# Matmul with batch normalisation on one core: the contraction dimension dealt to partitions in runs of eight, and the weight loaded block by block

## The chip, the core and the metric

The kernel runs on one core of one Trainium2 chip. The metric is the device time of one execution in microseconds (us), as the median of several runs. Before the change it is 205.72 us (three runs, 205.65 to 206.19).

Five engines work side by side: TensorE (PE, with its weight loads shown apart as PEld), VectorE (DVE), ScalarE (ACT), GpSimd (POOL) and SyncE (SP). Each works through its own queue of instructions in order. POOL and SP also issue the DMA transfers.

## The reference

```
y    = np.matmul(x, weight)            # x: 16 x 512 x 1024, weight: 1024 x 768, float32
mean = np.mean(y, axis=(0, 1), keepdims=True)
var  = np.var(y, axis=(0, 1), keepdims=True)
out  = gamma * (y - mean) / np.sqrt(var + eps) + beta
```

So 8192 rows of 1024 numbers (k) are multiplied by a 1024 x 768 matrix, and each of the 768 columns is normalised by its own mean and variance over all 8192 rows. No output can leave before the statistics of its column are complete.

## The kernel before

**Tiling.** The 8192 rows are 16 chunks of 512 (CH); a half chunk is 256 rows (QR). The contraction of 1024 is cut into 8 steps of 128 partitions: four blocks jw (JW = 4), each with two parities e. The 768 columns are six groups nt of 128. For nt 0 and 1 the product is made with rows on partitions (`rows_unit`, matmuls of line 510: x is the stationary operand, 256 columns of w move). For nt 2 to 5 it is made with columns on partitions (`col_unit`, line 575: w is stationary, x moves).

**How x gets its layout.** x comes in float32 and is cast to bf16 by the transfers that POOL issues (`load_x`, line 403): four transfers for each load, one for each quarter i of k, into partitions 32i to 32i+31 of the buffer `ring`. Each partition then holds 256 consecutive k of some rows. DVE transposes blocks of 32 x 32 (`turn_x`). For most chunks it moves pairs of bf16 numbers as one float32 word (line 435); for chunks 2, 3 and 6 (SINGLE) it moves single bf16 numbers and parts the two parities (line 428). Afterwards partition 32i + c holds k = 256 i + 64 jw + 2 c + e. In the source of the transpose the words of one block lie side by side (index c has step one word); for SINGLE the step of c is two bf16 numbers, also four bytes.

**How w gets its layout.** w must follow the same assignment of k. Since 32i + c maps to 256 i + ..., one transfer can fill only 32 partitions: `load_quarter` (line 387) loads quarter i of two blocks. There are eight such transfers: quarters 0 and 1 of blocks 0 and 1 first (`BETWEEN`, issued inside the first load of x), then the four transfers of x's rows 0 to 255, quarters 2 and 3 of blocks 0 and 1, x's rows 256 to 511, and the four quarters of blocks 2 and 3. Ahead of it, SP fetches one number from each of several rows of w (`touched`, line 350).

**The order around the change.** The order of instructions on every engine is made by a planner (`arrange`) that runs when the kernel is built. Every piece of work is a task with a due time, a modelled cost and its dependencies. The loads stand in the list `order` (line 440), and a POOL transfer waits until one of eight completion lanes is free. On PE the first chunk is taken in pieces: `part(0, 1, [0, 1])` multiplies rows 0 to 255 with blocks 0 and 1 (8 matmuls of line 510 and 16 of line 575); then one idle matmul pair (`FILL`, `wake`, line 591); then `part(1, 2, [0, 1])` the same for rows 256 to 511; then blocks 2 and 3 for all 512 rows. `WAKE` idle matmuls run before that from 1.5 us on. In the first chunk the transposes are split in two, blocks 0 and 1 and blocks 2 and 3.

**What follows.** From chunk 1 on each chunk takes 32 matmuls of line 510 and 32 of line 575, until the column groups are put off for some chunks. The sums of the row form are made by ACT (line 659, squares; line 672, the copy), DVE (line 662, sums; part of line 666) and POOL (the rest of line 666, sums of squares). The column form has its statistics in line 711 (DVE) and its copy in line 715 (ACT).

Of the kernel before, what the change touches and what calls it, by code (L numbers as in the profile page):

```python
# [227 lines left out]
def kernel(  # L228
# [9 lines left out]
    nc = tc.nc  # L238
# [5 lines left out]
    B, M0, K = x.shape  # L244
# [4 lines left out]
    NT = N // P  # L249
    KQ = K // 4  # L250
    CH = 512
# [4 lines left out]
    JW = KQ // 64  # L256
    PIECES = ((0,QR),(QR,QR))
    WAKE = 8
    FILL = 1
    SMALL = 8  # L260
    TOUCH = 1
    BETWEEN = {0: [0, 1]}
    EARLY = 4
    SHORT = 2
    GA = 2
# [27 lines left out]
    def seq(bi):  # L293

        ins = bi.ins
        prev = last.get(ins.engine)
        if prev is not None:
            tc.add_manual_dep(
                ins, prev,
                mybir.DependencyInfo(mybir.DependencyClass.NoSync, mybir.DependencyReason.DATA),  # L300
                reason="order",
            )
        last[ins.engine] = ins.name
        return bi
# [40 lines left out]

    seq(nc.scalar.activation(warm, eps_sb, AF.Sqrt))
    touched = singles.tile([P, 2, TOUCH], f32)
    first_rows = weight.rearrange("(i jw c e) n -> i c jw (e n)", i=4, jw=JW, e=2)
    for i in range(4):
        seq(nc.sync.dma_start(touched[32 * i:32 * i + 32, 0:2], first_rows[i, :, 0:2, 0:TOUCH]))  # L350


    tasks, turns = [], {}
# [2 lines left out]
    def task(prio, engines, emit, deps=(), lock=False, **kw):  # L356
        t = Task(prio, engines, emit, deps, **kw)
        t.lock = lock
        tasks.append(t)
        return t  # L360
# [19 lines left out]

    w_ready, x_ready, x_slot, plain, last_loads = {}, {}, {}, {}, []

    w_rows = weight.rearrange("(i jw c e) n -> i c jw (e n)", i=4, jw=JW, e=2)
    w_flat = w_sb.rearrange("p jw e n -> p jw (e n)")

    def load_quarter(i, jw, jw1):
        seq(nc.gpsimd.dma_start(w_flat[32 * i:32 * i + 32, jw:jw1], w_rows[i, :, jw:jw1]))  # L387

    def load_w(jw, jw1, quarters):
        def emit(eng):  # L390
            for i in quarters:
                load_quarter(i, jw, jw1)
        return emit

    def load_x(m0, rows, slot, between):
        def emit(eng):
            x_bf = piece(slot).bitcast(bf16).rearrange("p (t k) -> p t k", k=KQ)
            slot.tile = x_bf
            src = x_flat[m0:m0 + rows].rearrange("(t r) k -> r t k", r=32)
            for i in range(4):  # L400
                for quarter in between.get(i, ()):
                    load_quarter(quarter, 0, 2)
                bi = seq(nc.gpsimd.dma_start(x_bf[32 * i:32 * i + 32], src[:, :, KQ * i:KQ * (i + 1)]))  # L403
            slot.loader.ins = bi.ins
        return emit
# [11 lines left out]
    def turn_x(xslot, slot, m0, t0, jw0, jw1, new, rows=QR):  # L417
        def emit(eng):
            single = m0 // CH in SINGLE
            if new:  # L420
                xT_sb = xtpool.tile([P, JW, 2, CH] if single else [P, JW, CH, 2], bf16, tag="xT")
                slot.tile = xT_sb
            half, row = divmod((m0 + 32 * t0) % CH, QR)
            if single:
                src = xslot.tile[:, t0:t0 + rows // 32].rearrange("p t (jw c e) -> p t jw e c", jw=JW, e=2)
                dst = slot.tile[:, :, :, half * QR + row:half * QR + row + rows]
                dst = dst.rearrange("p jw e (t r) -> p t jw e r", r=32)
                seq(nc.vector.transpose(dst[:, :, jw0:jw1], src[:, :, jw0:jw1]))  # L428
                return
            src = xslot.tile[:, t0:t0 + rows // 32].rearrange("p t k -> p (t k)").bitcast(f32)  # L430
            src = src.rearrange("p (t jw c) -> p t jw c", jw=JW, c=32)
            dst = slot.tile.rearrange("p jw m e -> p (jw m e)").bitcast(f32)
            dst = dst.rearrange("p (jw q t r) -> p q t jw r", jw=JW, q=QPC, r=32)
            dst = dst[:, half, row // 32:(row + rows) // 32, jw0:jw1]
            seq(nc.vector.transpose(dst, src[:, :, jw0:jw1]))  # L435
        return emit

    for c in range(C):
        x_slot[c] = Slot(xts)
    order = [("x", 0), ("w", 0, 2), ("x", 1), ("w", 2, 4)]  # L440
    order += [("x", q) for q in range(2, SHORT * QPC)] + [("c", c) for c in range(SHORT, C - 1)]
    at = M - CH
    for rows in (CH-P,P):
# [3 lines left out]
    affine = None  # L447
    for kind, n, *n1 in order:
        if kind == "w":
            quarters = [i for i in range(4) if n > 0 or i not in sum(BETWEEN.values(), [])]  # L450
            took = len(quarters) * 192 * 4 * (n1[0] - n) / 4 * PER_KB * 1.024
            w_ready[n] = task(t, {"POOL": (0.535 * len(quarters), 0.535 * len(quarters))}, load_w(n, *n1, quarters), dma=took)
            w_ready[n].count = len(quarters)
            t += 2.1 * (n1[0] - n)
            if n1[0] == JW:
                idt = task(t, {"POOL": (0.6, 0.6)}, lambda eng: make_identity(nc, ident))
                task(t, act(0.25), lambda eng: seq(nc.scalar.copy(ident32, ident)), [idt])
            continue
        rows = n1[0] if kind == "p" else QR if kind == "x" else CH
        m0 = n if kind == "p" else n * rows  # L460
        if m0 == M // 2:
            affine_loads = affine = task(t, {"SP": (5.0, 7.0)}, load_affine, [x_ready[m0 // CH - 3, 0, JW]])
        slot = Slot(rings, rows // 32 * KQ // 2)
        between = BETWEEN if m0 == 0 else {}
        also = sum(len(v) for v in between.values())
        load = task(
            t, {"POOL": (2.68 * rows / CH + 0.535 * also, 2.68 * rows / CH + 0.535 * also)}, load_x(m0, rows, slot, between),
            dma=(rows * K * 4 / 1024 + 384 * also) * PER_KB * 1.024, takes=[slot])
        load.count = 4 + also
        slot.loader = load  # L470
        last_loads.append(load)
        t += 2.7 * rows / QR
        for i in range(rows // QR):
            c, q = divmod(m0 // QR + i, QPC)
            for j0, j1 in ((0, JW // 2), (JW // 2, JW)) if m0 < CH else ((0, JW),):
                new = q == 0 and j0 == 0
                x_ready[c, q, j1] = task(
                    -1000 + t, dve((2.2 if c in SINGLE else 1.16) * (j1 - j0) / JW + 0.02),
                    turn_x(slot, x_slot[c], m0, i * QR // 32, j0, j1, new), [load],
                    uses=[slot] if new else [slot, x_slot[c]], takes=[x_slot[c]] if new else [])  # L480
                if not new:
                    x_ready[c, q, j1].deps.append(x_ready[c, 0, JW // 2 if m0 < CH else JW])
            x_ready.setdefault((c, q, JW // 2), x_ready[c, q, JW])
        if rows % QR:
            t0 = rows // QR * QR // 32
            m1 = m0 + 32 * t0
            c, q = divmod(m1 // QR, QPC)
            x_ready["tile", m1 // P] = task(
                -1000 + t, dve(0.63), turn_x(slot, x_slot[c], m0, t0, 0, JW, False, P),
                [load, x_ready[c, 0, JW]], uses=[slot, x_slot[c]])  # L490
            x_ready[c, q, JW] = x_ready[c, q, JW // 2] = x_ready["tile", m1 // P]
# [95 lines left out]
    def wake(count, slot):  # L587
        def emit(eng):
            idle_ps = psum.tile([P, CH], f32, tag="b")
            for _ in range(count):  # L590
                seq(nc.tensor.matmul(idle_ps, idle_sb[:, 0:P], idle_sb, start=True, stop=True))  # L591
            small = idle_sb[:, 0:P // 2].bitcast(bf16)
            for _ in range(SMALL if count == WAKE else 0):
                seq(nc.tensor.matmul(idle_ps[:, 0:P], small, small, start=True, stop=True))
        return emit
# [5 lines left out]
    def pe_task(occ, emit, deps, key=None, **kw):  # L601
        t = task(clock[0], pe(occ), emit, deps, **kw)
        t.after = begun.get(key)
        begun[key] = t if key else None
        emit.task = t
        clock[0] += occ
        return t
# [166 lines left out]
    def part(q0, q1, jws):  # L774
        for h in range(q0, q1):
            rows_unit(0, [2 * h, 2 * h + 1], jws)
        for nt in range(GA, NT):
            col_unit(nt, 0, jws, q0, q1)

    part(0, 1, [0, 1])  # L780
    fill_slot = Slot(banks)
    pe_task(0.87 * FILL, wake(FILL, fill_slot), [w_ready[0]], takes=[fill_slot])
    part(1, 2, [0, 1])
    for h in range(2):
        rows_unit(0, [2 * h, 2 * h + 1], [2, 3])
    for nt in range(GA, NT):
        col_unit(nt, 0, [2, 3])

    halves = [range(JW // 2), range(JW // 2, JW)]
    merges = []  # L790
# [621 lines left out]
```

## Time and profile before

| | |
|---|---|
| median of three runs | 205.72 us (205.65 to 206.19) |
| span of the profiled execution, first to last instruction | 204.1 us |
| the rest of the median around that span | 1.6 us |
| mean granted PE clock over the span | 0.979 of full speed |
| HBM traffic | 36.71 MB read, 25.17 MB written |
| all loads of x have landed at about | 100 us |

The profile is of one execution; its time is given by its span, and the time around the span is taken as the difference to the median. "Busy" is the time in which an engine worked on an instruction. The chain of waits follows the last instruction back to what released it, step by step. "Releaser" is what ended an idle time. A transfer's "landing" is counted from its issue.

### The profile page before, as it was taken

The numbers are of one execution on the slowest core, as the hardware profiler recorded it, in microseconds if no ns is written. First come the engines' busy times: TensorE is split into PE (matmuls) and PEld (weight loads), VectorE is DVE, ScalarE is ACT, GpSimd is POOL, SyncE is SP. The second block draws the span as 40 slices with busy tenths as digits, with TensorE's granted clock in tenths as the row PEclk, the third lists the DMA queues.
The fourth block names the chain that finished last, engine by engine and source line by source line (L and its number), as shares of the span: only waits on it lengthen the run. The fifth ranks groups of instructions, "written<-read, shape, count | busy, mean of one in ns | idle before, by whom it ended". The sixth has DMA issues, their size and how long they took to land.

```text
span 204.1 us, 3510 instructions
## 1 busy us (share of the span) xinstructions
PE 189.3 (93%) x1210; PEld 114.5 (56%) x1210; DVE 159.3 (78%) x250; ACT 146.2 (72%) x260; POOL 124.1 (61%) x150
## 2 busy tenths in 40 slices
PE   7969999999999999999999999999999999997900
PEld 3457554657488888777865444444444445544600
DVE  4031879999999999969989998987999878657900
ACT  2001461368989999899978766999998959956950
POOL 7776954877499989997403999389613312940000
PEclk9999999999999999999999999999999999999965
DMA  4999999999999999999686899899999999999998
GB/s 71 172 199 196 176 196 196 196 197 197 190 193 197 197 196 196 196 197 195 103 181 200 297 339 336 248 301 328 295 322 227 336 303 274 347 343 310 310 347 253
DMA packets 98562, 48.74 MB, mean 239 GB/s; under 512 B 24304, under 2 KB 98032, under 8 KB 98544
## 3 DMA queue, kind: packets, MB, share of 16 engines
q0 software_dynamic: 34624, 18.36, 65.5%
q1 hardware_dynamic: 63920, 30.16, 52.6%
q8 instruction: 9, 0.15, 0.3%
q14 instruction: 9, 0.07, 0.1%
HBM read 36.71 MB, written 25.17 MB: 303 GB/s over the span
## 4 chain that ended last, share of the span: by engine, by line
PE 86%; ACT 3%; DMA 3%; POOL 2%; issue 1%; ACTq 0%; DVE 0%; POOLq 0%
PE y_ps L575 54%; PE y_ps L510 24%; PE y_ps L814 4%; ACT o_sb L1361 3%; DMA ring<-in_x_dram 3%; PE o_ps L1044 1%; POOL ring L403 1%; POOL w_sb L387 1%; PE y_ps L753 1%; PE a_ps L903 1%; PE o_ps L1074 0%; ACTq L1407 0%; PE idle_ps L591 0%; PE tot_ps L871 0%; ACT ring L1252 0%
## 5 line engine op out<-in xcount | busy, mean ns | idle before, releaser
L575 PEld LDWEIGHTS <-w_sb 128*128 128x128 bf16 x520 | 50.3, 97 | 57.6
L575 PE MATMUL y_ps<-xT_sb,w_sb 128*128 128x512 bf16 (+1 forms) x272 | 59.3, 371 | 0.0
L575 PE MATMUL y_ps<-x_pl,w_sb 128*128 128x512 bf16 x248 | 57.4, 379 | 0.0
L403 POOL DMA_DIRECT2D ring<-in_x_dram x76 | 47.2, 626 | 14.4 <-DMA ring<-in_x_dram 5.5
L510 PE MATMUL y_ps<-w_sb,xT_sb 128*128 128x256 bf16 x448 | 50.6, 273 | 1.7 <-DMA ring<-in_x_dram 1.6
L510 PEld LDWEIGHTS <-xT_sb 128*128 128x128 bf16 x448 | 43.5, 98 | 9.4 <-DVE xT_sb L435 2.9
L435 DVE STREAM_TRANSPOSE xT_sb<-ring 128x1024 f32<-128x1024 f32 (+1 forms) x29 | 31.2, 1111 | 14.1 <-DMA ring<-in_x_dram 13.9
L711 DVE BATCH_NORM_STATS2 stats<-y_ps 128x6 f32<-128x512 f32 x46 | 30.9, 687 | 7.7 <-PE y_ps L575 7.2
L715 ACT CAST y_sb<-y_ps 128x512 bf16<-128x512 f32 x51 | 29.0, 593 | 10.4 <-DVE stats L711 6.3
L547 ACT COPY x_pl<-xT_sb 128x1024 bf16<-128x1024 bf16 x32 | 32.8, 1063 | 1.7 <-DVE xT_sb L435 1.7
L942 POOL TENSOR_TENSOR ring<-ring,sum 128x1024 f32<-128x1024 f32 (+1 forms) x11 | 23.8, 2188 | 14.9 <-ACT y_ps L724 10.9
L659 ACT ACTIVATE sq_sb<-y_ps 128x512 f32<-128x512 f32 x28 | 16.3, 610 | 16.2 <-PE y_ps L510 15.9
L666 POOL TENSOR_TENSOR sum<-sum,sq_sb 128x512 f32<-128x512 f32 x20 | 25.6, 1278 | 3.0 <-ACT sq_sb L659 1.7
L662 DVE TENSOR_TENSOR sum<-y_ps,sum 128x512 f32<-128x512 f32 x28 | 18.9, 675 | 6.3 <-ACT sq_sb L659 5.3
L672 ACT CAST y_sb<-y_ps 128x512 bf16<-128x512 f32 x28 | 16.3, 594 | 8.2 <-DVE sum L662 8.0
L1178 POOL TENSOR_TENSOR ring<-ring,sum 128x1024 f32<-128x1024 f32 x6 | 14.8, 2477 | 9.8 <-issue 8.5
L937 DVE TENSOR_TENSOR ring<-y_sb,a_ps 128x1024 f32<-128x1024 bf16 (+1 forms) x16 | 16.7, 1079 | 0.1
L1044 PE MATMUL o_ps<-ident,y_sb 128*128 128x128 bf16 x104 | 13.1, 221 | 1.6 <-DVE y_sb L1348 1.5
L1232 ACT CAST ring<-ring 128x1024 f32<-128x1024 bf16 x13 | 13.8, 1063 | 0.6 <-DMA ring<-y_sb 0.6
L1145 POOL COPY sum<-sum 32x256 f32<-32x256 f32 (+1 forms) x17 | 5.8, 340 | 13.4 <-DVE sum L1142 6.5
L428 DVE STREAM_TRANSPOSE xT_sb<-ring 128x2048 bf16<-128x2048 bf16 x6 | 13.5, 2290 | 0.1
L591 PE MATMUL idle_ps<-idle_sb 128*128 128x512 f32 x18 | 9.6, 688 | 1.5 <-DVE idle_sb L316 1.5
(104 smaller groups left out, 153.7 us busy)
## 6 DMA issues: line engine op xcount, KB each, us to landing
out_dram<-ring SPq DMA_DIRECT2D x37, 512.0 KB, 3.4
ring<-in_x_dram POOLq DMA_DIRECT2D x52, 256.0 KB, 8.8
out_dram<-o_sb SPq DMA_DIRECT2D x6, 512.0 KB, 4.7
ring<-in_x_dram POOLq DMA_DIRECT2D x16, 128.0 KB, 5.9
w_sb<-in_weight_dram POOLq DMA_DIRECT2D x8, 192.0 KB, 6.2
out_dram<-ring SPq DMA_DIRECT2D x6, 256.0 KB, 3.0
ring<-in_x_dram POOLq DMA_DIRECT2D x4, 192.0 KB, 7.8
out_dram<-o_sb SPq DMA_DIRECT2D x3, 256.0 KB, 2.5
```

The source lines that it names most:

```text
L403: bi = seq(nc.gpsimd.dma_start(x_bf[32 * i:32 * i + 32], src[:, :, KQ * i:KQ * (i + 1)]))
L435: seq(nc.vector.transpose(dst, src[:, :, jw0:jw1]))
L510: seq(nc.tensor.matmul(y_ps[:, s], x_of(c, jw, e, t * P, (t + 1) * P), w_sb[:, jw, e, 0:NA], start=(s == 0 and jw == 0 and e == 0), stop=( ...
L547: seq(nc.scalar.copy(dst, pairs) if eng == "ACT" else ENG[eng].tensor_copy(dst, pairs))
L575: seq(nc.tensor.matmul(y_ps, w_sb[:, jw, e, nt * P:(nt + 1) * P], moving(c, jw, e, q0 * QR, q1 * QR, parted), start=(jw == 0 and e == 0 an ...
L659: seq(nc.scalar.activation(sq_sb[:, 0:n], slot.tile[:, 0:n], AF.Square))
L662: seq(nc.vector.tensor_add(sum1, slot.tile[:, 0:n], sum1))
L666: seq(ENG[eng].tensor_add(acc, acc, state["sq"][:, 0:n]))
L711: seq(nc.vector.bn_stats(dst, slot.tile))
L715: seq(nc.scalar.copy(y(nt, c), slot.tile))
L937: seq(nc.vector.tensor_mul(slot.o, y_row[c].y[:, s0:s1], aff[0][:, None, :].to_broadcast([P, n, NA])))
L942: seq(ENG[eng].tensor_add(slot.o, slot.o, row[:, None, :].to_broadcast([P, n, NA])))
```

## The change

k is dealt out anew: partition p holds k = 8 p + 2 jw + e. For w that gives every partition eight consecutive rows of the matrix, and a block jw is two of them, 6 KB in one piece. One transfer with all 128 partitions loads one block, and there are four such transfers. For x the transfers stay as they are, since 8 p with p = 32 i + c is 256 i + 8 c. The transposes pick other words: the index c now has a step of four words (16 bytes), or of eight bf16 numbers (16 bytes) in the SINGLE chunks. What they write is laid out as before.

The list of loads becomes block 0, x rows 0 to 255, block 1, x rows 256 to 511, block 2, block 3. PE takes rows 0 to 255 with block 0 and then with block 1, rows 256 to 511 with both, and then block 2 and block 3 each for all 512 rows. The idle pair between the parts is gone.

```
-    first_rows = weight.rearrange("(i jw c e) n -> i c jw (e n)", i=4, jw=JW, e=2)
+    w_rows = weight.rearrange("(p jw e) n -> p jw (e n)", jw=JW, e=2)
...
-    def load_quarter(i, jw, jw1):
-        seq(nc.gpsimd.dma_start(w_flat[32 * i:32 * i + 32, jw:jw1], w_rows[i, :, jw:jw1]))
-
-    def load_w(jw, jw1, quarters):
-        def emit(eng):
-            for i in quarters:
-                load_quarter(i, jw, jw1)
+    def load_w(jw):
+        def emit(eng):
+            seq(nc.gpsimd.dma_start(w_flat[:, jw], w_rows[:, jw]))
...
-                for quarter in between.get(i, ()):
-                    load_quarter(quarter, 0, 2)
...
-                src = xslot.tile[:, t0:t0 + rows // 32].rearrange("p t (jw c e) -> p t jw e c", jw=JW, e=2)
+                src = xslot.tile[:, t0:t0 + rows // 32].rearrange("p t (c jw e) -> p t jw e c", jw=JW, e=2)
...
-            src = src.rearrange("p (t jw c) -> p t jw c", jw=JW, c=32)
+            src = src.rearrange("p (t c jw) -> p t jw c", jw=JW, c=32)
...
-    order = [("x", 0), ("w", 0, 2), ("x", 1), ("w", 2, 4)]
+    order = [("w", 0), ("x", 0), ("w", 1), ("x", 1), ("w", 2), ("w", 3)]
...
-    part(0, 1, [0, 1])
-    fill_slot = Slot(banks)
-    pe_task(0.87 * FILL, wake(FILL, fill_slot), [w_ready[0]], takes=[fill_slot])
+    part(0, 1, [0])
+    part(0, 1, [1])
     part(1, 2, [0, 1])
-    for h in range(2):
-        rows_unit(0, [2 * h, 2 * h + 1], [2, 3])
-    for nt in range(GA, NT):
-        col_unit(nt, 0, [2, 3])
+    for jw in range(2, JW):
+        for h in range(2):
+            rows_unit(0, [2 * h, 2 * h + 1], [jw])
+        for nt in range(GA, NT):
+            col_unit(nt, 0, [jw])
```

The planner's cost for a transpose is left as it was. Its plan changes with the new tasks: two of DVE's additions of squares (line 666) go to POOL, POOL makes the identity matrix after the loads of x's rows 256 to 511 and not before them, and the order of statistics, copies and transposes shifts on DVE and ACT until about the last loads of x. After that, and on SP throughout, the order is the same.

## Prediction

> **What bounds it now.** I read the page first, then the windows, the chain of waits and the timeline of the first 30 us.
>
> ```profile
> span 204.1 us, 3510 instructions
> PE 189.3 (93%) x1210; PEld 114.5 (56%) x1210; DVE 159.3 (78%) x250; ACT 146.2 (72%) x260; POOL 124.1 (61%) x150
> ```
>
> The second line is from part 1 of the page: PE is busy 93% of the span. The window from 20 to 101 us says where it is not idle at all (columns: PE, PEld, DVE, ACT, POOL busy, each with its instructions, clock, DMA share, GB/s):
>
> ```profile
> 20.00:101.00 81.00, 80.94 (x600) 58.18 (x599) 74.69 (x87) 63.78 (x106) 65.03 (x86) 1.00 1.43 189
> ```
>
> PE lacks 0.06 us of 81, at full clock. DVE is the next one, with 6.3 us to spare. So a change at the start gains what it lets PE begin *without a break* earlier, and nothing after that. The timeline of the start shows what sets this point:
>
> ```profile
> 10.26 1.30 DVE L435 STREAM_TRANSPOSE xT_sb<-ring 128x512 f32<-128x512 f32 x2 [7.13 <-DMA ring<-in_x_dram]
> ...
> 12.14 1.03 PE L510 MATMUL y_ps<-w_sb,xT_sb 128*128 128x256 bf16 x8 [1.58 <-DMA ring<-in_x_dram]
> ...
> 14.85 1.30 DVE L435 STREAM_TRANSPOSE xT_sb<-ring 128x512 f32<-128x512 f32 x2 [3.28 <-DMA ring<-in_x_dram]
> 15.62 0.82 PEld L510 LDWEIGHTS <-xT_sb 128*128 128x128 bf16 x8 [0.60 <-DVE xT_sb L435]
> ...
> 18.58 1.66 PEld L510 LDWEIGHTS <-xT_sb 128*128 128x128 bf16 x16 [0.33 <-issue]
> ...
> 24.62 1.25 DVE L435 STREAM_TRANSPOSE xT_sb<-ring 128x1024 f32<-128x1024 f32 x1 [0.69 <-DMA ring<-in_x_dram]
> ...
> 25.92 1.64 PEld L510 LDWEIGHTS <-xT_sb 128*128 128x128 bf16 x16 [0.33 <-DVE xT_sb L435]
> ```
>
> Four gates follow each other. (1) 12.14: x's first rows were transposed from 10.26 on, but the last quarter of blocks 0 and 1, issued at 5.32 and landing 6.7 later, came at 12.0. (2) 15.62: rows 256 to 511 had landed at 14.8, and DVE needed 0.65 for half of them. (3) 18.58: the last quarter of blocks 2 and 3, issued at 12.29 with 6.2 to landing, came at 18.5. (4) 25.92: chunk 1's second half landed at 24.5 (issued 18.75, 5.7 to landing) and was transposed by 25.87. The chain of waits has "issue" for 0.07 us at 18.54 and 0.04 at 25.89: gates (3) and (4) are only just gates. The transfers themselves flow without a hole between 7 and 22 us:
>
> ```profile
> GB/s 0 0 31 111 206 152 91 180 206 209 189 194 193 218 217 203 202 186 190 194 193 192 144 171 179 196 197 196 195 196 196 196 195 197 196 197 196 196 198 195
> ```
>
> That is the DMA view of 0 to 40 us, 1 us a number (bytes written).
>
> **The change, step by step.** *Bytes and their order.* Block 0 (384 KB written) takes the place of the first two quarters of blocks 0 and 1 (part 6 of the page: 192 KB each); block 1 that of the next two; blocks 2 and 3 that of the last four. Each load thus ends at the same byte of the stream, and as the stream has no hole, at the same time: block 0 at 6.0 (2.0 issued + 4.0), x's first rows at 10.2, block 1 at 12.0, rows 256 to 511 at 14.8, block 2 at about 16.6, block 3 at 18.5, chunk 1 at 24.5. *Issue.* Eight transfers of w at 534 ns (the first 682) become four; 128 runs each lie between the 64 of a quarter (534) and the 256 of an x load (575), say 0.55. POOL saves 4.4 − 2.3 = 2.1 us by 13 us, hidden behind the stream. POOL makes the identity later (0.5 us); ACT's copy of it waits longer, but behind it stands only line 659, due at 21.6. The two additions that go to POOL stand ahead of chunk 3's loads, which go from 23.4 to about 25; in the stream chunk 2 lasts until 29.7. On SP the four small fetches (1.81 us) stay, and nothing is behind them.
>
> *PE.* Gate (1) becomes 10.26 + 0.65 = 10.95. Block 0 with the first rows is 12 matmuls, half of 0.87 + 1.81 (the rows of the chain for 8 and 16): 1.34, to 12.3; block 1 is there at 12.1; to 13.65. In the kernel before this part ends at 14.85, so 1.2 us are gained there. Gate (2) stays at 15.6 for want of x: the 1.2 us become idle time, 13.65 to 15.6, where the idle pair (0.86) stood. Then 2.68 to 18.35. Gate (3) goes, since block 2 is there since 16.6: 0.2 gained. Blocks 2 and 3 take (1.76 + 3.61) = 5.4, to 23.7; the first half of chunk 1 1.76, to 25.5; then gate (4), at 25.92 as before. The 0.4 us gained turn into a wait there. Sum on the path: **0.0 us**. What stands behind gate (4) on PE is all the rest, so from there on the runs are equal. The statistics of chunk 0 come nearer together (rows end at 21.5 and not 19.5), and about 0.7 us of DVE's sums go past 21.5; DVE is idle 2.3 us between 20 and 40, and PE needs no bank before 27.7.
>
> *The transposes.* They read words 16 bytes apart where the words lay side by side. No row shows such a read. The nearest rows, from the groups by shape up to 105 us:
>
> ```profile
> L435 DVE STREAM_TRANSPOSE xT_sb<-ring 128x1024 f32<-128x1024 f32 x23 | 27.4, 1224 | 3.7 <-DMA ring<-in_x_dram 3.5
> ...
> L428 DVE STREAM_TRANSPOSE xT_sb<-ring 128x2048 bf16<-128x2048 bf16 x6 | 13.5, 2290 | 0.1
> ...
> L435 DVE STREAM_TRANSPOSE xT_sb<-ring 128x512 f32<-128x512 f32 x6 | 3.9, 680 | 10.4 <-DMA ring<-in_x_dram 10.4
> ```
>
> (1224 − 680) / 512 = 1.06 ns an element for words side by side, and 2290 / 2048 = 1.12 for half words picked four bytes apart: the time goes by elements, whether or not the neighbours are wanted. That excludes a gain. I take **no change**, by line 428. The far ends: one more element time for each element, or (time by the bytes passed over) four times. There are 38,912 elements, 41.3 us: the ends are +41 and +124 us of DVE work. Of a doubling, 2.2 us fall on x's first rows, where DVE is idle (0.5 of it on the path); of the other 39.2, DVE's idle time from 20 to 102 us (its windows are busy 17.72 of 20, 18.86 of 20, 22.96 of 24 and 16.04 of 18: 6.4 idle) and the 1.5 us of additions given to POOL can take at most 7.9.
>
> **The rivals.** *The step is paid (slower).* If a word from another 16-byte stretch each time costs DVE twice, DVE takes over as the bound from 25 us on: 39.2 − 7.9 + 0.5 = 32, so **238 us**, and up to 245 if the idle time can't be used. It decides from a fifth on (7.9 of 39.2): below that it hides, at a third more it costs 12.9 − 7.9 = 5, 211 us. For it: DVE is busy 74.7 of 81 us, so there's hardly cover. Against it: line 428 pays nothing for skipping. The Trainium skill, "Advanced Engine Details and Errata", section Memory Cachelines, speaks for it: SBUF has lines of 16 bytes, two hits on a line are needed to absorb the access latency, and a different line at each access costs. No run here shows that: both transposes of the trace read four times from each 16 bytes, so it neither agrees nor differs.
>
> *The clock falls in the idle time.* Without the pair, PE rests 1.95 us. The break of 1.58 us before 12.14 left the clock at 1.00, but after the last matmul (ends 194.1) it fell inside this window:
>
> ```profile
> 194.00:196.00 2.00, 0.09 (x2) 0.00 (x0) 0.00 (x0) 2.00 (x4) 0.00 (x0) 0.92 1.15 346
> ```
>
> 0.92 as a mean of 1 and 0.5 over 2 us puts the fall at 195.7, some 1.6 us after. At the start the weight loads of the idle matmuls (timeline) follow at 0.86 us until 4.2 and at 0.43 from 4.8 on, so from 1.49 on it took about 3 us of work to get the clock up. Price: 3 us at half speed lose 1.5, less the 0.4 in hand at gate (4): +1.1, **206.8**. By the Trainium skill, "TensorE: Matmul & The Clock Gate", Part 1, it takes an idle window of about 3.4 us, and 1.95 would not do; the tail of this trace differs, with a fall 1.6 us after the last matmul.
>
> *The stream comes earlier.* At 5 and 6 us it moves 152 and 91 GB/s where 200 is usual: 157 KB, 0.8 us. If transfers over all 128 partitions fill this dip, every gate comes 0.8 us earlier: **204.9**. Against it: in the dip x's first rows are moved, whose transfers stay as they are.
>
> **How the numbers follow.** Forecast, the stream is the gate as before: 205.72 + 0.0 = 205.7, own range 205.1 to 206.3, chance 0.44. The profiled span of 204.1 should come again; the 1.6 us around it are the difference to the median. The step paid in full 0.32 (238 to 245), in part 0.06 (about 211), the clock 0.08 (206.8), the earlier stream 0.10 (204.9). A measurement of this kernel can tell about 0.3%, 0.6 us, from no change. Faster by more: 0.10 and 0.02 of the forecast's edge, 0.12. Within: 0.39. Slower: 0.32 + 0.06 + 0.08 + 0.03 = 0.49. Signs are thus nearly even, with one case likeliest and another far away. The range takes in all but the ends, 0.06 above and 0.04 below: 204.8 to 243.
>
> **What would show it.** Right: PE's first matmuls near 10.95, an idle time near 13.7 to 15.6 released by DVE, no wait at 18.4, a wait at about 25.5 to 25.9, and PE's window from 26 to 101 as full as before; the 128x1024 transposes near 1224 ns and the bf16 ones near 2290. Wrong: these rows at 2300 and 4460 with PE waiting for line 435 all through (the step is paid); a granted clock below 1 between 13 and 22 us; loads of x landing before 14.2 and 24.0. What I hold for surest is that the loads of x, not w, gate PE from 15 us on; what I know least is the price of the 16-byte step, and it alone could move the time by more than 2 us.

## The result and the profile after

The changed kernel takes 228.62 us (median of four runs, 228.54 to 228.86) beside 205.78 for the kernel before on the same chip: a ratio of 1.1104, interval 1.1076 to 1.1132. It is slower by 22.8 us. The profiled execution agrees: its span is 226.8 us where it was 204.1, 22.7 more. Line numbers of the changed kernel are lower: nine less in the loads and transposes, 14 less from line 510 on (435 is now 426, 428 is 419, 510 is 496, 575 is 561, 662 is 648, 666 is 652, 715 is 701, 403 is 394).

Part 1 of the page after:

```profile
span 226.8 us, 3499 instructions
PE 197.0 (87%) x1208; PEld 115.9 (51%) x1208; DVE 186.3 (82%) x248; ACT 147.2 (65%) x260; POOL 124.9 (55%) x148
```

DVE works 27.0 us longer (159.3 before) with two instructions fewer. PE shows 7.7 us more for the same work less one idle pair, and is idle 29.8 us instead of 14.8. The windows after say where (columns as before: PE, PEld, DVE, ACT, POOL busy, each with its instructions, clock, DMA share, GB/s):

```profile
20.00:40.00 20.00, 17.87 (x114) 10.73 (x113) 17.59 (x14) 7.54 (x14) 13.00 (x17) 1.00 1.37 184
40.00:60.00 20.00, 16.46 (x89) 8.76 (x87) 19.90 (x18) 8.66 (x14) 11.96 (x17) 0.91 1.17 150
60.00:84.00 24.00, 21.09 (x163) 16.52 (x162) 23.69 (x20) 16.93 (x28) 15.16 (x19) 0.93 1.19 144
84.00:102.00 18.00, 13.83 (x107) 10.86 (x106) 17.47 (x16) 13.89 (x22) 13.91 (x16) 0.91 1.29 164
102.00:126.00 24.00, 21.08 (x157) 14.51 (x154) 23.70 (x25) 19.71 (x37) 13.64 (x21) 1.00 0.98 148
```

PE was full from 20 to 101 us; now it lacks 15.7 us of the 106 between 20 and 126, while DVE lacks 3.7 and is full from 40 us on. The bound has changed hands. It is the transposes that grew, as the groups by shape up to 130 us show (count, busy us, mean ns, idle time before):

```profile
L426 DVE STREAM_TRANSPOSE xT_sb<-ring 128x1024 f32<-128x1024 f32 x23 | 46.1, 2043 | 4.5 <-DMA ring<-in_x_dram 4.5
L419 DVE STREAM_TRANSPOSE xT_sb<-ring 128x2048 bf16<-128x2048 bf16 x6 | 22.9, 3872 | 0.0
...
L426 DVE STREAM_TRANSPOSE xT_sb<-ring 128x512 f32<-128x512 f32 x6 | 6.2, 1071 | 9.4 <-DMA ring<-in_x_dram 9.4
```

1224 ns became 2043, 2290 became 3872, 680 became 1071. By (2043 − 1071) / 512 an element now costs 1.90 ns where it cost 1.06. In all DVE has 23 x 0.819 + 6 x 1.582 + 6 x 0.391 = 30.7 us more to do. (The 27.0 of the page is less: DVE makes two additions fewer, and where two rows overlap, as 83.22 + 4.06 and 87.19 below, the page counts that time once.) One stretch of DVE's timeline shows the new rhythm (start, length, engine and line, what it writes and reads, count):

```profile
83.22 4.06 DVE L426 STREAM_TRANSPOSE xT_sb<-ring 128x1024 f32<-128x1024 f32 x2
87.19 2.25 DVE L648 TENSOR_TENSOR sum<-y_ps,sum 128x512 f32<-128x512 f32 x3
89.35 0.68 DVE L652 TENSOR_TENSOR sum<-sum,sq_sb 128x512 f32<-128x512 f32 x1
89.95 3.98 DVE L426 STREAM_TRANSPOSE xT_sb<-ring 128x1024 f32<-128x1024 f32 x2
```

One chunk costs DVE 6.7 us, with no hole. With the old transposes the same work would take 2 x 1.22 + 2.25 + 0.68 = 5.4 us, while two chunks on PE lay 5.65 us apart in the kernel before at this place (rows of line 510 began at 85.41 and 91.06). So PE, which used to set the pace by a little, now waits. The chain that ended last, by engine, says the same (PE had 86% of it before):

```profile
PE 39%; DVE 28%; DMA 12%; issue 11%; ACT 4%; POOL 2%; ACTq 0%; DVEq 0%; POOLq 0%
```

DVE's share is the transposes and sums of that rhythm. In the waits from 10 to 130 us (engine, line, what it waits for: us, times, longest) PE's weight loads and its matmuls wait for line 426; and POOL's loads of x wait too, because the buffer `ring` comes free late, so that the transfers thin out (150 and 144 GB/s from 40 to 84 us in the windows above, 194 and 196 before):

```profile
POOL ring L394 <- DVE xT_sb L419: 15.2, 3, 6.3
...
PEld L496 <- DVE xT_sb L426: 10.2, 8, 3.1
...
PE y_ps L496 <- DVE xT_sb L426: 7.7, 5, 2.8
```

The start, which most of the prediction was about, went nearly as it said (timeline of the start, after):

```profile
11.78 0.60 PE L496 MATMUL y_ps<-w_sb,xT_sb 128*128 128x256 bf16 x4
...
14.62 2.06 DVE L426 STREAM_TRANSPOSE xT_sb<-ring 128x512 f32<-128x512 f32 x2 [2.40 <-DMA ring<-in_x_dram]
15.76 1.05 PE L496 MATMUL y_ps<-w_sb,xT_sb 128*128 128x256 bf16 x8 [1.13 <-DVE xT_sb L426]
...
25.08 2.00 DVE L426 STREAM_TRANSPOSE xT_sb<-ring 128x1024 f32<-128x1024 f32 x1
27.14 1.92 PE L496 MATMUL y_ps<-w_sb,xT_sb 128*128 128x256 bf16 x16 [1.42 <-DVE xT_sb L426]
```

x's rows 256 to 511 landed at 14.5 (forecast 14.8), block 3 of w at 18.3 (18.5), chunk 1's second half at 24.4 (24.5). The third gate, the wait at 18.5, is gone. The rest of the start is the longer transposes again: chunk 1's second half is transposed at 27.08, not 25.87.

### The profile page after: what moved, and what is told of

Same layout as the page of the kernel before. It is cut to its first block, busy times and chain, and to the rows that moved or that the text cites. A ratio compares the mean times of both kernels' runs of the same rounds, so it can differ in the third digit from the quotient of the medians.

```text
span 226.8 us, 3499 instructions
## 1 busy us (share of the span) xinstructions
PE 197.0 (87%) x1208; PEld 115.9 (51%) x1208; DVE 186.3 (82%) x248; ACT 147.2 (65%) x260; POOL 124.9 (55%) x148
## 4 chain that ended last, share of the span: by engine, by line
PE 39%; DVE 28%; DMA 12%; issue 11%; ACT 4%; POOL 2%; ACTq 0%; DVEq 0%; POOLq 0%
PE y_ps L561 34%; DVE xT_sb L426 15%; DMA ring<-in_x_dram 8%; DVE xT_sb L419 5%; DVE sum L648 4%; DMA w_sb<-in_weight_dram 4%; ACT o_sb L1347 3%; PE y_ps L800 2%; DVE sum L652 1%; PE o_ps L1030 1%; DVE stats L697 1%; POOL ring L394 1%; PE y_ps L739 1%; ACT y_sb L701 1%; POOL w_sb L385 1%
## 5 line engine op out<-in xcount | busy, mean ns | idle before, releaser
L496 PE MATMUL y_ps<-w_sb,xT_sb 128*128 128x256 bf16 x448 | 55.5, 283 | 12.8 <-DVE xT_sb L426 7.7
L426 DVE STREAM_TRANSPOSE xT_sb<-ring 128x1024 f32<-128x1024 f32 (+1 forms) x29 | 52.2, 1842 | 13.9 <-DMA ring<-in_x_dram 13.9
L561 PE MATMUL y_ps<-xT_sb,w_sb 128*128 128x512 bf16 (+1 forms) x272 | 61.3, 377 | 2.2 <-ACT y_sb L701 2.2
L496 PEld LDWEIGHTS <-xT_sb 128*128 128x128 bf16 x448 | 44.7, 102 | 24.2 <-DVE xT_sb L426 10.2
L652 POOL TENSOR_TENSOR sum<-sum,sq_sb 128x512 f32<-128x512 f32 x22 | 28.2, 1280 | 9.7 <-ACT sq_sb L645 9.0
L928 POOL TENSOR_TENSOR ring<-ring,sum 128x1024 f32<-128x1024 f32 (+1 forms) x11 | 23.7, 2194 | 17.4 <-ACT y_ps L710 13.3
L658 ACT CAST y_sb<-y_ps 128x512 bf16<-128x512 f32 x28 | 16.4, 587 | 14.2 <-DVE sum L648 14.0
L419 DVE STREAM_TRANSPOSE xT_sb<-ring 128x2048 bf16<-128x2048 bf16 x6 | 22.9, 3872 | 0.0
L1030 PE MATMUL o_ps<-ident,y_sb 128*128 128x128 bf16 x104 | 13.1, 221 | 1.6 <-DVE y_sb L1334 1.5
```

The costliest lines, as they stand in the source:

```text
L496: seq(nc.tensor.matmul(y_ps[:, s], x_of(c, jw, e, t * P, (t + 1) * P), w_sb[:, jw, e, 0:NA], start=(s == 0 and jw == 0 and e == 0), stop=( ...
L561: seq(nc.tensor.matmul(y_ps, w_sb[:, jw, e, nt * P:(nt + 1) * P], moving(c, jw, e, q0 * QR, q1 * QR, parted), start=(jw == 0 and e == 0 an ...
L652: seq(ENG[eng].tensor_add(acc, acc, state["sq"][:, 0:n]))
L928: seq(ENG[eng].tensor_add(slot.o, slot.o, row[:, None, :].to_broadcast([P, n, NA])))
```

## The experiments

The theory: the whole loss is the price of reading words 16 bytes apart, paid on DVE, which has no room for it. The rivals: that the price depends on how far the step goes (bytes passed over), or on what else uses SBUF at the time; that the four transfers of w and the new order have a part in the loss; and that PE's lower granted clock (0.91 to 0.93 from 40 to 102 us) carries some of it.

### The step by itself

A kernel that holds only transposes and copies of 1024 elements, in which the step of the reads goes from 4 to 64 bytes; in the rows shown below one instruction runs after the other, with all else at rest:

```diff
+    nc.vector.transpose(to_f32, f32_at(1))  # f32 read step 4 bytes
+    nc.vector.transpose(to_f32, f32_at(2))  # f32 read step 8 bytes
+    nc.vector.transpose(to_f32, f32_at(3))  # f32 read step 12 bytes
+    nc.vector.transpose(to_f32, f32_at(4))  # f32 read step 16 bytes
...
+    nc.vector.transpose(to_f32, f32_at(16))  # f32 read step 64 bytes
...
```

> Leaves the whole computation out: it only times transposes of 1024 elements (and plain copies on DVE, ACT and POOL) from SBUF, one after the other, with the read step varied; the output is constant. Theory 1 (DVE pays for a new 16-byte stretch of SBUF at each element): float32 transposes at steps of 4 and 8 bytes take 1.06 ns an element above the fixed 0.14 us (about 1.22 us), at 16 bytes and all wider steps the same 1.9 ns (about 2.04 us), 12 bytes in between; bf16 at 4 bytes as at 2, at 16 bytes 1.84 ns. Theory 2 (time goes by the bytes passed over): 8 bytes about 1.5 us, 16 bytes 2.04, 32 bytes 3.7, 64 bytes 7. Theory 3 (what is paid is not the step but the load on SBUF from PE, ACT and DMA in the full kernel): here, with those engines idle, 16 bytes costs 1.22 us as well.

Its timeline, of one execution (each form stands in the kernel twice, and the two agree within 0.1 us; shown is the second. Lines 82 to 84 read bf16 at steps of 4, 8 and 16 bytes; 72 to 75 read float32 at 4, 8, 12 and 16 bytes, 78 at 64; 87 and 90 are DVE's copy at 4 and 16, 93 and 96 ACT's, 99 and 102 POOL's):

```profile
51.40 1.19 DVE L82 STREAM_TRANSPOSE to_bf<-words 128x1024 bf16<-128x1024 bf16 x1
...
53.09 1.22 DVE L83 STREAM_TRANSPOSE to_bf<-words 128x1024 bf16<-128x1024 bf16 x1
...
54.82 1.95 DVE L84 STREAM_TRANSPOSE to_bf<-words 128x1024 bf16<-128x1024 bf16 x1
...
80.75 1.25 DVE L72 STREAM_TRANSPOSE to_f<-words 128x1024 f32<-128x1024 f32 x1 [16.60 <-POOL to_f L71]
82.03 1.25 DVE L73 STREAM_TRANSPOSE to_f<-words 128x1024 f32<-128x1024 f32 x1
83.31 1.53 DVE L74 STREAM_TRANSPOSE to_f<-words 128x1024 f32<-128x1024 f32 x1
84.87 1.98 DVE L75 STREAM_TRANSPOSE to_f<-words 128x1024 f32<-128x1024 f32 x1
...
90.95 1.90 DVE L78 STREAM_TRANSPOSE to_f<-words 128x1024 f32<-128x1024 f32 x1
...
96.18 0.69 DVE L87 COPY to_f<-words 128x1024 f32<-128x1024 f32 x1
...
98.51 1.07 DVE L90 COPY to_f<-words 128x1024 f32<-128x1024 f32 x1
...
100.73 1.04 ACT L93 COPY to_f<-words 128x1024 f32<-128x1024 f32 x1 [27.98 <-DVE to_f L91]
...
104.53 1.99 ACT L96 COPY to_f<-words 128x1024 f32<-128x1024 f32 x1
...
108.64 1.04 POOL L99 COPY to_f<-words 128x1024 f32<-128x1024 f32 x1 [27.92 <-ACT to_f L97]
...
112.48 1.99 POOL L102 COPY to_f<-words 128x1024 f32<-128x1024 f32 x1
```

DVE's transpose pays nothing at 8 bytes, a part at 12, everything at 16, and no more at 64. bf16 does the same by bytes, not by elements: 1.19 us at 4 bytes, 1.22 at 8, 1.95 at 16. So it is neither the distance nor the number of elements skipped, nor traffic of others, since there was none. What fits is the count of numbers taken from each stretch of 16 bytes: two are enough, one costs. The price is not DVE's alone: ACT and POOL pay 0.95 us for 1024 elements as well. A step of 32 bytes in what a transpose writes costs as much (2.00, line 86).

The Trainium skill, "Advanced Engine Details and Errata", section Memory Cachelines, says this: lines of 16 bytes, and two hits on a line to absorb the latency. This run agrees (1.25 at 8 bytes, 1.98 at 16). The price here is 0.73 us for 1024 elements.

### The step alone in the kernel

The kernel before with the two lines that choose the words, and nothing else of the change:

```diff
-                src = xslot.tile[:, t0:t0 + rows // 32].rearrange("p t (jw c e) -> p t jw e c", jw=JW, e=2)
+                src = xslot.tile[:, t0:t0 + rows // 32].rearrange("p t (c jw e) -> p t jw e c", jw=JW, e=2)
...
-            src = src.rearrange("p (t jw c) -> p t jw c", jw=JW, c=32)
+            src = src.rearrange("p (t c jw) -> p t jw c", jw=JW, c=32)
```

> The kernel before with the two lines of the transposes changed alone: they read words 16 bytes apart, and so x's numbers meet the wrong rows of w; loads, their order and PE's order are those of before. Theory 1 (the step alone): 128x1024 transposes at 2.04 us, bf16 at 3.87, and the time of the changed kernel, 227 to 230 us. Theory 2 (the new loads, the PE order and its idle time take part, with the clock): the step by itself gives 215 to 224 us. Theory 3 of the probe (load on SBUF from the 128-partition transfers): close to 206.

228.48 us (228.34 to 228.49), ratio 1.1101 (1.1085 to 1.1118), which is the whole change's ratio. Its groups by shape:

```profile
L435 DVE STREAM_TRANSPOSE xT_sb<-ring 128x1024 f32<-128x1024 f32 x23 | 46.0, 2033 | 0.0
...
L428 DVE STREAM_TRANSPOSE xT_sb<-ring 128x2048 bf16<-128x2048 bf16 x6 | 22.9, 3848 | 0.0
```

### Everything but the step

The kernel after with the old reading, so that its order of instructions is that of the kernel after on every engine:

```diff
-                src = xslot.tile[:, t0:t0 + rows // 32].rearrange("p t (c jw e) -> p t jw e c", jw=JW, e=2)
+                src = xslot.tile[:, t0:t0 + rows // 32].rearrange("p t (jw c e) -> p t jw e c", jw=JW, e=2)
...
-            src = src.rearrange("p (t c jw) -> p t jw c", jw=JW, c=32)
+            src = src.rearrange("p (t jw c) -> p t jw c", jw=JW, c=32)
```

> The changed kernel with the old reading of the transposes: words side by side, so x's numbers meet the wrong rows of w; loads by block, PE's order and the removed idle pair are those of the change. Theory 1: transposes at 1.22 and 2.29 us, gates as the prediction had them (first matmuls near 10.95 us, an idle time from 13.7 to 15.6, chunk 1's second half near 25.9), and 205.7 us, within 0.6 of before. Theory 2: 208 us or more, with the granted clock under 1 between 13 and 22 us or PE idle after 26 us.

205.98 us (205.54 to 206.48), ratio 1.001 (1.000 to 1.0021), span 204.0. This is the prediction's forecast of no change, met by all of the change but the step. Its timeline of the start has the gates as they were forecast, at 10.95, 15.6 and 25.9:

```profile
11.15 0.60 PE L496 MATMUL y_ps<-w_sb,xT_sb 128*128 128x256 bf16 x4
...
15.27 1.05 PE L496 MATMUL y_ps<-w_sb,xT_sb 128*128 128x256 bf16 x8 [1.27 <-DVE xT_sb L426]
...
25.76 1.92 PE L496 MATMUL y_ps<-w_sb,xT_sb 128*128 128x256 bf16 x16 [0.53 <-DVE xT_sb L426]
```

At 11.15 PE came from its own idle matmuls, though: x's first rows were transposed by 10.65. There is no wait at 18, PE is full from 40 to 102, and the clock is 1.00 from 10 to 20 us. So the rivals that give the transfers or the order a part in the loss fall.

### The new order with the old layout

The loads and PE's order of the changed kernel, but k dealt out as before, so that a block of w takes four transfers over 32 partitions each (16 in all):

```diff
-            seq(nc.gpsimd.dma_start(w_flat[:, jw], w_rows[:, jw]))
+            for i in range(4):
+                seq(nc.gpsimd.dma_start(w_flat[32 * i:32 * i + 32, jw], w_rows[i, :, jw]))
...
```

> A complete kernel: the old assignment of k, so the transposes read side by side, with the change's order of blocks in loads and matmuls; each block of w comes in four transfers of a quarter (sixteen in all, not eight). Theory 1: 205.7 us as before, since x's loads are the gate; sixteen issues of 0.53 us are hidden behind the stream. Rival: POOL's issue (8.5 us for w) or the eight lanes hold x's loads up, chunk 1's second half lands after 25 us, and it is 0.5 to 2 us slower.

208.64 us (208.23 to 209.9), ratio 1.0147 (1.0123 to 1.0172). x's rows 256 to 511 land at 15.1 (14.4 in the kernel above), chunk 1's second half at 26.9 (24.3), and the stream has dips: 69 and 100 GB/s at 5 and 6 us, 134 and 125 at 18 and 19 (127 and 112, 193 and 194 in the kernel above). This is the rival that was expected, larger than its 0.5 to 2 us: POOL's issue, or its eight lanes, hold the loads up. From 10 to 20 us POOL is busy 9.12 us (row below; 5.73 in the kernel above). An issue takes 0.51 us for 96 KB, which is 194 GB/s at most; from 13.3 to 15.4 us one follows the other at 0.69, which is 142, and about 4.3 us later (the median time to landing) come the 134 and 125. The 32 partitions alone don't do it: the kernel before also fills 32 at a time, with 192 KB, and its stream moves 180 GB/s or more from 7 to 21 us. And here a break on PE was long enough for the clock to fall. Timeline, and the window around it:

```profile
16.00 1.89 PE L498 MATMUL y_ps<-w_sb,xT_sb 128*128 128x256 bf16 x8 [1.97 <-DVE xT_sb L427]
17.68 2.81 PE L563 MATMUL y_ps<-xT_sb,w_sb 128*128 128x256 bf16 x16
```

```profile
10.00:20.00 10.00, 8.03 (x56) 5.65 (x55) 2.61 (x4) 0.00 (x0) 9.12 (x18) 0.83 1.18 177
```

Eight matmuls take 1.89 us for 1.05, sixteen 2.81 for 1.98: 1.7 us lost. So the new layout of w does have a use, that a block comes in one issue. With the old layout the same order costs 2.9 us.

The Trainium skill, "TensorE: Matmul & The Clock Gate", Part 1, has the clock fall after an idle window of about 3.4 us, and calls the window free-running. This trace differs in the length: 1.97 us did it here, while 1.13 (kernel after) and 1.27 (above) left the clock at 1.00.

### A step of 8 bytes

The kernel before with k = 256 i + 128 h + 4 c + 2 j + e, so that two words of each 16 bytes are taken:

```diff
-    w_rows = weight.rearrange("(i jw c e) n -> i c jw (e n)", i=4, jw=JW, e=2)
+    w_rows = weight.rearrange("(i h c f) n -> i h c (f n)", i=4, h=2, f=4)
...
-            src = src.rearrange("p (t jw c) -> p t jw c", jw=JW, c=32)
+            src = src.rearrange("p (t h c j) -> p t h j c", h=2, c=32, j=2)
```

> The kernel before with k dealt as 256 i + 128 h + 4 c + 2 j + e (block jw = 2 h + j): the transposes read words 8 bytes apart (index c, both in the float32 and in the bf16 form) and write as before; the transfers of w stay eight, each partition of one now reads 12 KB in one piece instead of twice 6 KB. Order and everything else as before. Theory 1 (the price belongs to reads that use a 16-byte stretch only once; two words from each are enough): transposes of 1024 words near 1225 ns, of 2048 bf16 numbers near 2290 ns (for these the probe shows 1.22 against 1.19 us for 1024 at 8 bytes), and 205.7 us within 0.6. Rival (any step away from side by side costs in this kernel, where DVE reads while transfers write): 1024 words at 1.5 us or more, at least 33 times 0.3 = 10 us more DVE work, and 209 us or more. If pieces of 12 KB also help the first loads, up to 0.4 us less.

206.40 us (205.81 to 207.46), ratio 1.0029 (1.001 to 1.0047). Groups by shape:

```profile
L435 DVE STREAM_TRANSPOSE xT_sb<-ring 128x1024 f32<-128x1024 f32 x23 | 27.5, 1227 | 3.7 <-DMA ring<-in_x_dram 3.6
...
L428 DVE STREAM_TRANSPOSE xT_sb<-ring 128x2048 bf16<-128x2048 bf16 x6 | 13.5, 2287 | 0.2 <-DMA ring<-in_x_dram 0.2
```

The transposes are as they were without a step, in the busy kernel too. The 0.3% are not theirs: the loads of x land some 0.35 us later in this profile (first transpose at 10.62 for 10.26), and PE carries that to the end (span 204.6). Pieces of 12 KB for w did not help.

### The step in a part of the chunks

Twice the kernel before, with the step only in the bf16 transposes (chunks 2, 3 and 6), and only in the float32 ones (all other chunks); the edits are the first and the second pair of lines shown for the step alone.

> The kernel before with the 16-byte step in the bf16 transposes alone (chunks 2, 3 and 6; their x numbers meet other rows of w than they should). The dose: 6 times (3.85 - 2.29) = 9.4 us more DVE work, all of it between 25 and 60 us. If DVE's idle time anywhere up to 102 us (6.4) takes it up, 9.4 - 6.4 = 3.0 more, 208.8 us. If only what is idle up to about 60 us counts (2.3 + 1.1 = 3.4), because PE has no idle time later to catch up in, 9.4 - 3.4 = 6.0 more, 211.8 us. If DVE were not the bound in the changed kernel, nothing: 205.8.

> The kernel before with the 16-byte step in the float32 transposes alone (all chunks but 2, 3 and 6, whose reading is as before; the numbers of x in the others meet other rows of w than they should). 23 x 0.81 + 6 x 0.39 = 21.0 us more DVE work. If the parts add up (both 22.7 more, the bf16 part alone 7.9): 14.8 more, 220.6 us, within 1. If each part alone loses nearly its whole work, because DVE's idle time before a loss does not count: 21.0 less about 2, 224 to 225.

The bf16 part takes 213.74 us (213.47 to 214.23), ratio 1.0379 (1.0353 to 1.0404): 7.9 us for 9.4 us of work (6 x (3859 − 2290) ns). The float32 part takes 219.35 (219.06 to 219.64), ratio 1.0651 (1.0631 to 1.0671): 13.4 for 21.0. Together 21.3, near the 22.7 of both; the 220.6 within 1 that was expected if the parts add up is missed by a little.

The first of these corrects how I counted cover. Both numbers that were expected, 208.8 and 211.8, were too low. Its windows:

```profile
20.00:40.00 20.00, 18.91 (x117) 11.23 (x118) 17.88 (x15) 7.25 (x14) 11.80 (x17) 1.00 1.41 189
40.00:60.00 20.00, 16.07 (x83) 8.41 (x83) 19.90 (x20) 11.48 (x19) 13.09 (x17) 0.91 1.26 157
60.00:84.00 24.00, 24.00 (x212) 20.48 (x210) 23.59 (x27) 20.36 (x34) 18.75 (x23) 1.00 1.33 166
84.00:102.00 18.00, 16.51 (x133) 12.70 (x132) 14.90 (x19) 16.49 (x26) 16.51 (x21) 1.00 1.45 196
```

DVE's idle time from 20 to 40 us is still there (2.1 us, 2.3 before): it is DVE waiting for x to land, and no work can be put into it. From 40 to 84 us it fell from 2.2 to 0.5: these 1.7 us are about all that hid (9.4 − 7.9 = 1.5). DVE's idle time after 84 us came too late for a loss that PE had by then. And it is followed by a second loss of 1.5 us from 84 to 102, where DVE itself waits for loads that went out late.

### The clock, and DVE's work

Two versions of the kernel after, both with the order unchanged on every engine but for the first's added matmuls. One gives PE idle matmuls where it waits, the other takes work off DVE:

```diff
+                if c > 0 and ts[0] == 0:
+                    seq(nc.tensor.matmul(y_ps, idle_sb[:, 0:P], idle_sb, start=True, stop=True, skip_group_check=True))
```

> The kernel after with one idle matmul of 128 x 512 on PE ahead of chunk 1 and of each of the next eleven chunks, where PE waits for DVE; the order of all other instructions is the same on every engine. Theory (DVE alone sets the pace; that the granted clock lies at 0.91 to 0.93 between 40 and 102 us is a consequence): the clock there goes up to 0.95 or more, and the time stays at 228.6 within 0.7. Rival (the lower clock carries part of the loss; PE was busy 7.7 us longer for the same matmuls): 2 to 7 us less, 222 to 227.

```diff
-            seq(nc.vector.tensor_add(sum1, slot.tile[:, 0:n], sum1))
+            seq(nc.vector.tensor_add(sum1[:, 0:32], slot.tile[:, 0:32], sum1[:, 0:32]))
```

> The kernel after, in which line 648 on DVE adds only 32 of 512 columns (the rest of that sum is left out); the order on every engine is the same. Each of the 28 additions should take about 0.18 us for 0.69, so DVE has 28 x 0.51 = 14 us less to do, 24 of them (12 us) by 126 us. Theory (DVE's work sets the pace between 25 and 126 us): 11 to 14 us less, 215 to 218 us, with the transposes as long as before (2.04 and 3.87 us). Rival (not DVE's work but the transposes' own length, through buffers and the time from a landing to PE, or PE's lower clock): less than half of that, 222 us or more.

The first takes 232.24 us (231.68 to 232.9), 3.6 more than the kernel after and not what either theory said. But it answers the question until 109 us. Its windows, and then a line of its DVE timeline:

```profile
60.00:84.00 24.00, 24.00 (x173) 17.41 (x172) 23.69 (x20) 17.00 (x28) 15.17 (x20) 1.00 1.21 147
84.00:102.00 18.00, 15.08 (x116) 11.15 (x115) 17.48 (x16) 13.69 (x21) 13.72 (x16) 1.00 1.24 159
```

```profile
103.44 4.08 DVE L426 STREAM_TRANSPOSE xT_sb<-ring 128x1024 f32<-128x1024 f32 x2
```

The clock is at 1.00 from 60 us on, where it was 0.93 and 0.91 (from 40 to 60 it stayed at 0.91, with DVE busy 19.90 of 20 in both kernels), and DVE's transposes stand where they stood (103.44; 103.30 in the kernel after). PE's slow clock lost nothing that PE didn't have to wait for anyway. The 3.6 come later, 2.4 of them here: at 111.49 an idle matmul pair of 1.02 us ran where PE had not been waiting, and the last pair of transposes but one began at 118.19 for 115.79. It is the last of 13 such pairs, one more than the twelve expected.

The second takes 217.59 us (217.46 to 218.46), 11.0 less than the kernel after, for 28 x (687 − 180) = 14.2 us of DVE work less, all of it before 122 us (I had expected 24 of the 28 there). Most of the other 3.2 us is new idle time of DVE: 0.7 from 20 to 40 us, 0.8 from 84 to 102 and 1.1 from 102 to 126 (16.89, 16.68 and 22.59 busy). The transposes are as long as before (groups by shape):

```profile
L426 DVE STREAM_TRANSPOSE xT_sb<-ring 128x1024 f32<-128x1024 f32 x23 | 46.4, 2054 | 5.5 <-DMA ring<-in_x_dram 5.5
...
L648 DVE TENSOR_TENSOR sum<-y_ps,sum 128x32 f32<-128x32 f32 x28 | 5.1, 180 | 2.9 <-ACT sq_sb L645 1.6
```

So it is DVE's sum of work that sets the pace, whichever instruction it comes from, and not the length of a transpose between a landing and PE.

### Two tries at a faster kernel

Chunk 1 in two halves (kernel before), so that gate (4) has work ahead of it; and, from the kernel after with the old layout and w in quarters, w's block 0, then all 512 rows, then blocks 1, 2 and 3, with the halves as well:

```diff
-    for c in range(1, RC):
+    for q in range(QPC):
+        rows_unit(1, [2 * q, 2 * q + 1])
+        for nt in range(GA, NT):
+            col_unit(nt, 1, range(JW), q, q + 1)
+    for c in range(2, RC):
```

```diff
-    order = [("w", 0), ("x", 0), ("w", 1), ("x", 1), ("w", 2), ("w", 3)]
+    order = [("w", 0, 1), ("x", 0), ("x", 1), ("w", 1, 2), ("w", 2, 4)]
...
```

> The kernel before with chunk 1 multiplied in two halves (rows and columns of its first 256 rows, then of the second 256), which is only an order on PE and what hangs on it. If the second half's landing gates PE at 25.9 us, PE has 3.6 us of work with the first half and none of the wait: 0.05 to 0.4 less, 205.3 to 205.7. If the gate is only just met, 205.7 within 0.3. A loss of 0.3 or more would mean that the column groups cost more in halves (256 instead of 512 moving columns for each weight load).

> A try at a faster kernel: the old layout (words side by side), w's block 0 in four quarters of one block, then x's rows 0 to 255 and 256 to 511, then blocks 1, 2 and 3 in quarters; PE takes block 0 with both halves and then one block after the other for all 512 rows, and chunk 1 in two halves. By the bytes, all 512 rows would be in 2 us earlier than now (384 KB less ahead of them), PE could run without a break from about 13.6 us with 1.3 us done before, and with 2.9 done by 15.6 now that is 0.5 to 1.6 less: 204.1 to 205.3. Rival: the quarters in pieces of 6 KB over 32 partitions slow the stream, as in order_only, and what is won by 35 us is lost again by the end, as in halves: 206 to 208.

The halves take 207.14 us (206.88 to 207.55), ratio 1.0057 (1.0037 to 1.0078). PE begins chunk 2 at 34.66 for 34.91, a gain of 0.25; at 184.6 us nothing is left of it. The column groups cost 0.2 us more in halves (2 x 3.79 for 7.39), which isn't the loss. It stands behind the engines' work: ACT ends its last copy at 196.7 in both kernels, and the stores that are left end the span at 205.5 for 204.1. The last 64 transposes on PE take 6.08 us for 5.50, but they take 6.12 in the kernel without the step as well, with a span of 204.0. What made the stores longer, and where the quarter of a microsecond went, these runs don't settle. The other kernel takes 207.77 (206.44 to 208.4), ratio 1.0102 (1.0078 to 1.0126), in the range of its rival. Its profile is of the fastest of its runs, 206.44: rows 256 to 511 are in at 13.1, but blocks 2 and 3 come at 18.9 and PE waits 0.86 us for them at 19.0. Neither beats the kernel before.

## Why the prediction was wrong

**The step that failed** is the one on the transposes: "I take **no change**, by line 428." Line 428 in the kernel before skips every second bf16 number and costs nothing for it, and I read this as "the time goes by elements, whether or not the neighbours are wanted". But a step of four bytes still takes four numbers from each 16 bytes. The row was near in form and far in the one thing that mattered. The probe has both sides: 1.19 us at 4 bytes, 1.95 at 16. The text itself said that both transposes of the trace "read four times from each 16 bytes", and that no run could speak on the rule; a row that can't speak on it could not be the row to choose by.

**The mechanism of the first rival was right**, its size too large. The sign that the text had named for it came, float32 transposes at 2043 and bf16 ones at 3872 (for 2300 and 4460), with PE waiting for them all through. "One more element time" of 1.06 ns was 0.80 (float32) and 0.77 (bf16): 30.7 us of DVE work, not 41.3. With these prices the prediction's own sum takes off the four transposes of x's first rows (1.6 us, about 0.4 of it on the path) and the cover of 7.9: 30.7 − 1.6 − 7.9 + 0.4 = 21.6 us, for 22.8 measured. That it comes so near is partly luck, since two errors work against each other: the rows count more work than there is, and the cover is too wide. From 20 us to the end of the transposes DVE was busy 75.6 of 82 us before and is busy 101.3 of 105 after (windows 20 to 102 and 20 to 125). That is 25.8 us more work, where the rows come to 30.7 − 1.6 − 1.5 (additions) = 27.6, and only 2.8 of the 6.4 us of idle time are filled: most of the rest is DVE waiting for x (17.72 of 20 busy from 20 to 40 us before, 17.59 after), where no work can be put.

**The gates were right.** "Sum on the path: 0.0 us" for the transfers and the order is 205.98 beside 205.77 in the kernel without the step, with the first matmul at 11.15 (10.95), the second gate at 15.27 (15.6), no third, and the fourth at 25.76 (25.92). That the loads of x and not w gate PE from 15 us on was right. That four transfers replace eight bought nothing, as the bytes ahead of each load are the same and the stream has no new dip. (Equal bytes alone are not enough: with sixteen transfers chunk 1's second half came 2.6 us later.) Two slips in the sums change nothing: 10.26 + 0.65 is 10.91, and a third of 39.2 is 13.1.

**The clock** did not fall in the break before 15.6 us, which was 1.13 us in the kernel after and 1.27 without the step, and not 1.95: idle matmuls ahead of it and the later first part made it shorter. The mechanism exists, though: a break of 1.97 us did it in one kernel (1.7 us lost; I had priced it at 1.5). The 3 us of work behind that price are no fixed figure: from 1.49 on, the weight loads of the same idle matmuls halved their distance after 3.3 us in the kernel before, 4.9 without the step and 6.0 in the kernel after. **The stream** did not come 0.8 us earlier: it moves 123 and 122 GB/s at 5 and 6 us in the kernel after, a dip as before, and without the step DVE begins on x's rows 256 to 511 at 14.50 for 14.85 and on chunk 1's second half at 24.46 for 24.62.

**The chances.** Slower had the largest share, 0.49, and the case that held most of it, 0.32, gave 238 to 245. The forecast stood on the case that needed no price; the unknown price was the whole question, and two of its three bounds meant a loss of tens of microseconds with an engine that had 6 us to spare.

## What to carry to other kernels

When a layout is changed, count how many elements each engine takes from every 16 bytes of SBUF: two were free here, one cost 1.6 to 1.7 times the transposes and 1.9 times the copies on ACT and POOL. Saved transfers are paid once, at the start; a dearer access is paid at every chunk, so set it against the room of the engine that makes it, and count as room only idle time that is not itself a wait for data and that comes before the loss. An engine at 92% of a stretch beside a full one is a bound in waiting: 0.82 us more on each of its transposes made it the bound.

## What the runs showed of the hardware

- The price of a 16-byte step in reads, for 1024 float32 elements, from a step of 4 bytes: DVE's transpose 1.25 to 1.98 us, DVE's copy 0.69 to 1.07, ACT's copy 1.04 to 1.99, POOL's 1.04 to 1.99. At 8 bytes DVE pays nothing, ACT and POOL 0.07 and 0.05 (1.11, 1.09); at 12 it is a part (1.53, 0.84, 1.55, 1.52). Above 16 at most 0.03 is added, to 64 bytes for the transpose and to 32 for the copies. Writes were tried at 32 bytes alone, on DVE and ACT, and cost the same (2.00, 1.07 and 2.02).
- PE's clock can fall in breaks of 1.5 to 2 us: it did at 1.97, it did not at 1.13, 1.27 and 1.58. Before the last 64 transposes on PE a break of 1.53 us left it at 0.98 over the next 8 us in the kernel before, and at 0.79 in the kernel with halves.
- The same idle matmuls, begun at 1.49 us, came to double speed after 3.3 to 6.0 us, differently in each profile (by the distance of their weight loads: before 3.3, order_only 4.4, no_step 4.9, after 6.0). The granted clock of the window from 0 to 10 us is 1.00 in all four.
- Sixteen transfers of 96 KB put deeper dips into the stream than four of 384 KB (69 and 134 GB/s for 127 and 193 at 5 and 18 us; order_only and no_step, in which the order of loads by block is the same): chunk 1's second half lands at 26.9 instead of 24.3. An issue on POOL takes 0.51 us for 96 KB and 0.57 for 384, so small transfers bound the rate. Their number, size and partitions were not varied one at a time.
